# A feed-forward kernel whose weight sums move from GpSimd to VectorE, and whose residual comes in half tiles

## The chip, the cores and the metric

The kernel runs on one core of a Trainium2 chip. The metric is the device time of one execution in microseconds (us), as the median of several runs. The core's engines are TensorE (PE in the profile, its weight loads PEld), VectorE (DVE), ScalarE (ACT), GpSimd (POOL) and SyncE (SP, which here only issues DMAs). Each engine takes its instructions in order from a queue of its own and waits where an instruction's input isn't there or the buffer that it writes isn't free. A DMA is issued from the queue of an engine, in that engine's order.

## The reference, cut to what matters

One layer (`DEPTH = 1`): a spatial-gating mixer and a cross-attention side by side, a projection, a LayerNorm with a scaled residual, then a SwiGLU feed-forward with another residual and LayerNorm. Only the feed-forward and its residual bear on the change.

```python
D_MODEL = 1024; SEQ = 2048; D_FF = 2816
DEEPNORM_ALPHA = (2 * DEPTH) ** 0.25

def swiglu_ffn(x, w_in, w_down):
    h = x @ w_in
    return (jax.nn.silu(h[..., :D_FF]) * h[..., D_FF:]) @ w_down

x = layer_norm(DEEPNORM_ALPHA * x + branch @ w_o[i], ln1_g[i], ln1_b[i])
x = layer_norm(DEEPNORM_ALPHA * x + swiglu_ffn(x, ffn_w_in[i], ffn_w_down[i]), ln2_g[i], ln2_b[i])
```

## The kernel before

**Numbers.** Every operand of a matmul is split into a high part and the rest: `split` (L70 to L74) casts it on ScalarE to the type of TensorE's inputs (L73, the high part) and subtracts the result from it on VectorE (L74, the low part). Each product is then three matmuls (`PASSES`: high by high, high by low, low by high). So no weight reaches TensorE before ScalarE and VectorE have both worked on it. Blocks of 2 by 2 submatrices are multiplied with seven products in place of eight; this needs sums of the submatrices made ahead, on both sides, and sums of the products behind.

**Passes and blocks.** The feed-forward works on the tokens in three passes of 688, 680 and 680 (`FPASSES`), each in two halves of `h` = 344 or 340. The 2816 hidden features are 22 columns f of 128, taken in five blocks: 5, 4, 4, 4, 5 of them in pass 0, and 4, 4, 4, 4, 6 in passes 1 and 2 (`FBLOCKS`). For each f, `up(f)` multiplies x by w1 (84 matmuls of 128x344 or 128x340, tile `h`); behind the products 5, 7, 3 and 4 VectorE takes the results out of PSUM (L401, L402, L392, L396), and the result `c` is split into `g`. After its columns, the block's part of the product with w2 is added to the output tiles `fa`.

**The products with w2.** In pass 0, `down` does this with plain products (tile `d`). In passes 1 and 2, the first four blocks use seven products (`down7`, tile `e`, weights `w_e`). What these need of w2 is made once, in pass 0, by the generator `left_sums` (L484): for each of the first four blocks (`blk`) and each pair of output rows (`m` = 0, 2, 4, 6), 16 tiles in all. One tile is worked on during each `up(f)` of pass 0 from f = 5, a step behind each product. Its steps are: two DMAs from GpSimd's queue load the tile `r_es..m` (L481, in `tiles4`); four sums of 128x256 into `s_es..m` (L493); then for each of two parts a split (L73, L74) and a store to device memory from GpSimd's queue (L499, `k_e`). `r_es` and `s_es` share the pool `g` with the tiles g, 7 buffers.

**The residual.** In passes 1 and 2, `down7` adds the residual in its fourth block (`last`), since the fifth block is done by `down`. This is in `second(j)`, for j = 0 to 3: an add of a common part into the output tile (L531, L532), then for each of two row tiles m a load of x1d (128x680, tile `r_fr`, L538, SP's queue) into the pool tag `raw`, and `fa = ALPHA * r + fa` on VectorE (L539). The tag `raw` has 4 buffers (L66, `raw`) and serves nearly every weight that is loaded, among them `r_u_17_0`, the weight of `up(17)`, the first work of TensorE behind the fourth block. The pool `tmp` (L888) has 9 buffers of 128 by `h`; each `up(f)` takes five of them:

```python
def tmp(self, name):
    return open_pools["tmp"].tile([P, self.h], F32, tag="tmp", name=f"{name}_{self.no}")

m1, u2, c12, c21, c22 = (self.tmp(f"{x}_{f}") for x in ("m1", "u2", "c12", "c21", "c22"))
```

**What sets the order.** The program is written by a framework whose scheduler puts each engine's instructions in an order from its own estimates; only the order of TensorE is fixed by hand (`in_order`). An edit of one instruction can move others on every engine.

Of the kernel before, what the change touches and what calls it, by code (L numbers as in the profile page):

```python
# [14 lines left out]
ALU = mybir.AluOpType  # L15
AX = mybir.AxisListType

P = 128
# [16 lines left out]
ALPHA = 2.0 ** 0.25  # L35
# [4 lines left out]
def trunk_kernel(ctx, tc, xT, memT, wv, wuq, ws, bs, vg, vb, wmk, wmv, wo,  # L40
                 ln1g, ln1b, w1, w2, ln2g, ln2b, outT):
    nc = tc.nc
# [16 lines left out]
    def matmul(*args, **kw):  # L59
        in_order(nc.tensor.matmul(*args, **kw))  # L60
# [4 lines left out]
    def bank(name):  # L65
        return psum.tile([P, 512], F32, tag="bank", name=name)  # L66

    def raw(shape, name):
        return common.tile(shape, F32, tag="raw", bufs=4, name=name)

    def split(hi, lo, src, engine=nc.vector):

        nc.scalar.copy(hi, src)  # L73
        engine.tensor_sub(lo, src, hi.bitcast(F32))  # L74
# [109 lines left out]
    x1d = dram.tile([D, SEQ], F32, tag="x1d", name="x1d")  # L184
# [160 lines left out]
    class Pass:  # L345
# [138 lines left out]
        def left_sums(self, blk, m, f0, q):  # L484

            name, key = f"es{blk}_{m}", f"e{blk}_{m}"
            r, s = (open_pools["g"].tile([P, 4, q, P], F32, tag="g", name=f"{x}_{name}") for x in "rs")
            v = self.tiles4(m, f0, q, name, r.rearrange("p (a i) j x -> p a (i j) x", a=2))
            yield
            a11, a12, a21, a22 = (v[:, a, j] for a in range(2) for j in range(2))  # L490
            for n, (x, y, op) in enumerate(((a21, a22, ALU.add), (s[:, 0], a11, ALU.subtract),
                                            (a11, a21, ALU.subtract), (a12, s[:, 1], ALU.subtract))):
                nc.gpsimd.tensor_tensor(out=s[:, n], in0=x, in1=y, op=op)  # L493
                yield
            for pa, k, to in ((5, slice(0, 2), r), (7, slice(2, 4), s)):
                hl = to.bitcast(F32R)
                split(hl[:, 0:2], hl[:, 2:4], s[:, k])
                t = kept[f"{key}_{pa}"] = dram.tile([P, 4, q, P], F32, tag=f"{key}_{pa}", name=f"k_{key}_{pa}")
                nc.gpsimd.dma_start(out=t, in_=to)  # L499
                yield  # L500

        def down7(self, blk, q, f0, last, w):

            h, n, gp = self.h, self.n, self.gp
            if blk == 0:
                self.u = [open_pools["sums"].tile([P, 4, P], F32, tag="sums", name=f"fu{self.no}_{m}")
                          .rearrange("p a b -> p (a b)")[:, 0:h] for m in range(0, KD, 2)]
            banks = []

            def product(j, p):  # L510
                y, u = self.out[j], self.u[j]
                c11, c12, c21, c22 = (y[:, a, b * h:(b + 1) * h] for a in range(2) for b in range(2))
                n, start, stop = {1: (0, True, False), 6: (1, True, True), 2: (0, False, True), 5: (2, True, False),
                                  7: (3, True, False), 3: (2, False, True), 4: (3, False, True)}[p]
                bk = banks[j][n]
                for i in range(q):
                    for x, (a, b) in enumerate(PASSES):
                        matmul(bk, w[j][p][:, a, i, :], gp[p][:, i, b], start=start and i == 0 and x == 0,
                               stop=stop and i == q - 1 and x == 2, skip_group_check=True)
                to = {1: u, 6: u, 2: c11, 5: c22, 7: c22, 3: c12, 4: c21}[p]  # L520
                if blk == 0 and p not in (1, 7):
                    nc.scalar.copy(to, bk)
                else:
                    nc.vector.tensor_add(to, to, bk)

            def second(j):
                for p in (2, 3, 4):
                    product(j, p)
                if last:
                    y, u = self.out[j], self.u[j]  # L530
                    nc.vector.tensor_add(y[:, 0, h:n], y[:, 0, h:n], u)  # L531
                    nc.vector.tensor_tensor(out=y[:, 1].rearrange("p (b t) -> p b t", b=2),  # L532
                                            in0=y[:, 1].rearrange("p (b t) -> p b t", b=2),
                                            in1=u.unsqueeze(1).broadcast_to([P, 2, h]), op=ALU.add)
                    for m in range(2):
                        r = raw([P, n], f"r_fr{self.no}_{j}_{m}")
                        m0 = (2 * j + m) * P
                        nc.sync.dma_start(out=r, in_=x1d[m0:m0 + P, self.t0:self.t0 + n])  # L538
                        nc.vector.scalar_tensor_tensor(out=y[:, m], in0=r, scalar=ALPHA, in1=y[:, m],  # L539
                                                       op0=ALU.mult, op1=ALU.add)  # L540

            for j in range(KD // 2):
                if j < KD // 2 - 1:
                    w.append(self.left(blk, 2 * j + 2, f0, q))
                banks.append([bank(f"e{i}_{self.no}_{blk}_{j}")[:, 0:h] for i in range(4)])
                for p in (6, 1, 5, 7):
                    product(j, p)
                if j:
                    second(j - 1)
            second(KD // 2 - 1)  # L550

        def sums(self):
# [427 lines left out]
    for no in range(len(FPASSES)):  # L980
        pa, h, n = ffn, FPASSES[no] // 2, FPASSES[no]
# [136 lines left out]
```

## Time and profile before

| | |
|---|---|
| Median of three runs | 2203.02 us |
| The three runs | 2204.48, 2203.02, 2201.71 us |
| The profiled execution | 2201.52 us, span 2199.7 us |
| Mean granted clock of TensorE | 0.987 |
| DMA | 408.12 MB, mean 186 GB/s |
| Costliest group: the `h` matmuls | 5544 of mean 322 ns, 892.5 us |

The span is the time from the first to the last instruction in the trace. The profile lists for each group of instructions the line of the source, the engine, the operation, the tile written and the tiles read (without their numbers), with count, busy time and the idle time just before them, and what ended it. In a timeline a row is a run of equal instructions: start, length from the first start to the last end, what it is, how many, and in brackets the idle time before it and who ended it. Names after an arrow are who was waited for. A row `DMA r_es<-in_w` says that the landing of that load was awaited.

### The profile page before, as it was taken

How to read it: one execution, taken by the hardware profiler on the slowest of the kernel's cores; microseconds unless marked ns; L12 is line 12 of the kernel's file. 1: busy time of each engine (PE TensorE's matmuls, PEld its weight loads, DVE VectorE, ACT ScalarE, POOL GpSimd, SP SyncE). 2: the span in 40 equal slices, each digit the busy share in tenths (PEclk: the TensorE clock that was granted, in tenths of full speed). 3: DMA queues.
4: the chain of work that ended last, by engine and by line, in shares of the span. 5: the costliest groups of instructions: out<-in, count | busy, mean ns of one | idle time of the engine just before them, and what ended most of it. 6: DMA issues, size and time to landing. Idle time of an engine off the chain costs nothing.

```text
span 2199.7 us, 35087 instructions
## 1 busy us (share of the span) xinstructions
PE 2097.4 (95%) x12938; PEld 1983.4 (90%) x12938; DVE 1591.2 (72%) x2950; ACT 921.4 (42%) x1846; POOL 419.8 (19%) x382
## 2 busy tenths in 40 slices
PE   9999999999999989999999999999989999999896
PEld 7888798798788879998999999999989999999896
DVE  7987796797788795776767875666757765666656
ACT  5553743654465452433424445332224353223234
POOL 1412321331322441213222320000002300000002
PEclk9999999999999999999999999999999999999998
DMA  6233324234334555767667558666674576666752
GB/s 211 77 115 125 106 79 161 91 97 147 118 96 132 187 198 217 256 207 275 215 227 276 168 198 268 222 227 229 224 246 141 197 262 236 231 230 218 249 168 94
DMA packets 156299, 408.12 MB, mean 186 GB/s; under 512 B 15328, under 2 KB 41952, under 8 KB 156128
## 3 DMA queue, kind: packets, MB, share of 16 engines
q1 hardware_dynamic: 135808, 333.50, 45.5%
q10 hardware_dynamic: 12672, 46.14, 5.4%
q0 software_dynamic: 7648, 26.24, 3.5%
q8 instruction: 102, 1.67, 0.3%
q14 instruction: 69, 0.57, 0.1%
HBM read 326.13 MB, written 79.69 MB: 184 GB/s over the span
## 4 chain that ended last, share of the span: by engine, by line
PE 62%; DVE 16%; DMA 8%; ACT 5%; issue 5%; POOL 4%; SPq 0%; ACTq 0%; DVEq 0%; POOLq 0%
PE h L60 30%; PE d L60 10%; PE e L60 9%; PE v L60 5%; PE y L60 4%; PE u L60 3%; DMA r_es<-in_w 2%; DMA r_x<-in_xT 2%; DVE w L74 1%; POOL s_es L493 1%; DVE w_u L74 1%; DVE w_o L74 1%; POOL s_a L233 1%; POOL s_b L233 1%; ACT p L743 1%
## 5 line engine op out<-in xcount | busy, mean ns | idle before, releaser
L60 PE MATMUL h<-x,w 128*128 128x340 f32 (+1 forms) x5544 | 892.5, 322 | 48.2 <-DVE c L401 17.2
L60 PEld LDWEIGHTS h<-x,w 128*128 128x128 f32 x5544 | 876.9, 190 | 59.6 <-ACT w L73 31.9
L60 PE MATMUL d<-g,w_d 128*128 128x344 f32 (+3 forms) x1632 | 264.0, 322 | 8.4 <-DVE g L74 3.6
L60 PEld LDWEIGHTS d<-g,w_d 128*128 128x128 f32 x1632 | 257.9, 189 | 12.7 <-DVE g L74 5.3
L60 PE MATMUL y<-br,w_o 128*128 128x512 f32 x960 | 224.2, 395 | 0.0
L60 PEld LDWEIGHTS y<-br,w_o 128*128 128x128 f32 x960 | 180.6, 189 | 41.7
L60 PE MATMUL e<-gp,w_e 128*128 128x340 f32 x1344 | 211.4, 318 | 0.0
L60 PEld LDWEIGHTS e<-gp,w_e 128*128 128x128 f32 x1344 | 209.9, 188 | 0.5 <-DVE w_e L74 0.2
L73 ACT CAST w<-r_u 128x512 fp32r<-128x512 f32 x198 | 121.8, 618 | 191.1 <-PE h L60 126.2
L60 PE MATMUL v<-w_v,x 128*128 128x512 f32 x768 | 187.8, 401 | 6.6 <-ACT w_v L73 4.8
L74 DVE TENSOR_TENSOR w<-r_u,w 128x512 fp32r<-128x512 f32 x198 | 144.2, 730 | 53.9 <-ACT w L73 46.6
L60 PEld LDWEIGHTS v<-w_v,x 128*128 128x128 f32 x768 | 143.5, 190 | 42.1 <-ACT w_v L73 4.8
L369 POOL TENSOR_TENSOR t<-r_f,r_f 128x340 f32<-128x340 f32 (+1 forms) x12 | 13.4, 1113 | 441.2 <-DVE c L392 377.0
L60 PE MATMUL u<-xt,w_u 128*128 128x256 f32 x768 | 97.1, 282 | 0.0
L60 PEld LDWEIGHTS u<-xt,w_u 128*128 128x128 f32 x768 | 94.3, 191 | 0.0
L60 PE MATMUL u<-x,w_u 128*128 128x256 f32 x576 | 79.5, 290 | 10.5 <-DVE u L709 5.2
L73 ACT CAST w_d<-r_d 128x384 fp32r<-128x384 f32 (+2 forms) x104 | 53.0, 519 | 76.4 <-PE d L60 50.7
L74 DVE TENSOR_TENSOR w_o<-r_o,w_o 128x512 fp32r<-128x512 f32 (+1 forms) x96 | 69.3, 732 | 21.4 <-ACT w_o L73 21.4
L60 PEld LDWEIGHTS u<-x,w_u 128*128 128x128 f32 x576 | 72.9, 193 | 13.1 <-issue 5.1
L74 DVE TENSOR_TENSOR w<-s_u,w 128x512 fp32r<-128x512 f32 x88 | 67.6, 775 | 22.0 <-ACT w L73 20.2
L73 ACT CAST gp<-c 128x340 fp32r<-128x340 f32 x112 | 51.8, 476 | 74.6 <-DVE c L398 42.0
L400 DVE TENSOR_TENSOR u<-h,m 128x340 f32<-128x340 f32 (+1 forms) x66 | 33.7, 511 | 66.9 <-PE h L60 65.9
(212 smaller groups left out, 2901.1 us busy)
## 6 DMA issues: line engine op xcount, KB each, us to landing
w<-k_u SPq DMA_DIRECT2D x176, 512.0 KB, 4.3
r_u<-in_w SPq DMA_DIRECT2D x88, 512.0 KB, 3.7
k_u<-w ACTq DMA_DIRECT2D x88, 512.0 KB, 3.3
r_u<-in_wuq SPq DMA_DIRECT2D x32, 512.0 KB, 3.3
r_o<-in_wo SPq DMA_DIRECT2D x32, 512.0 KB, 3.5
r_e<-in_w SPq DMA_DIRECT2D x64, 256.0 KB, 3.2
w_e<-k_e SPq DMA_DIRECT2D x64, 256.0 KB, 3.6
w_e<-k_e SPq DMA_DIRECT2D x32, 512.0 KB, 4.3
```

Of the source, the lines that this page charges most:

```text
L60: in_order(nc.tensor.matmul(*args, **kw))
L73: nc.scalar.copy(hi, src)
L74: engine.tensor_sub(lo, src, hi.bitcast(F32))
L233: nc.gpsimd.tensor_add(self.s2, self.s2, sq)
L369: nc.gpsimd.tensor_sub(t3, b22, b12)
L400: stages = {1: lambda: nc.scalar.copy(m1, q0), 6: lambda: nc.vector.tensor_add(u2, q1, m1), 2: lambda: nc.scalar.activation(m1, q0, AF.Sil ...
L493: nc.gpsimd.tensor_tensor(out=s[:, n], in0=x, in1=y, op=op)
L743: nc.scalar.activation(pr[:, h, :], svs[h // 2][:, h % 2, :], AF.Exp, scale=HD ** -0.5, bias=mxv[:, h:h + 1], accum_out=sm[:, h:h + 1])
```

## The change

Two edits. The four sums of `left_sums` are made by VectorE in place of GpSimd; the loads and stores of these tiles stay in GpSimd's queue. And in `second`, each residual tile of 128x680 in `raw` becomes two half tiles of 128x340 in `tmp`, each with its own load and its own instruction of VectorE. Lines from L540 on move down by two.

```diff
             for n, (x, y, op) in enumerate(((a21, a22, ALU.add), (s[:, 0], a11, ALU.subtract),
                                             (a11, a21, ALU.subtract), (a12, s[:, 1], ALU.subtract))):
-                nc.gpsimd.tensor_tensor(out=s[:, n], in0=x, in1=y, op=op)
+                nc.vector.tensor_tensor(out=s[:, n], in0=x, in1=y, op=op)
                 yield
...
                     for m in range(2):
-                        r = raw([P, n], f"r_fr{self.no}_{j}_{m}")
                         m0 = (2 * j + m) * P
-                        nc.sync.dma_start(out=r, in_=x1d[m0:m0 + P, self.t0:self.t0 + n])
-                        nc.vector.scalar_tensor_tensor(out=y[:, m], in0=r, scalar=ALPHA, in1=y[:, m],
-                                                       op0=ALU.mult, op1=ALU.add)
+                        for x in range(2):
+                            r, t0 = self.tmp(f"r{m}{x}_{j}"), self.t0 + x * h
+                            nc.sync.dma_start(out=r, in_=x1d[m0:m0 + P, t0:t0 + h])
+                            to = y[:, m, x * h:(x + 1) * h]
+                            nc.vector.scalar_tensor_tensor(out=to, in0=r, scalar=ALPHA, in1=to,
+                                                           op0=ALU.mult, op1=ALU.add)
```

The order of the instructions moves with it. First VectorE in pass 0, in the block of f = 9 to 12, beside the tile of m = 4. In the names, `c_11` is the result of `up(11)`, `r_es_4` and `s_es_4` are the tile of m = 4, `w_0_12` are weights of `up(12)`, and `s_u` sums for them. Before:

```order
L74 TENSOR_TENSOR w_0_11_9971<-r_u_11_1_9843,w_0_11_9971 128x512
L135 TENSOR_TENSOR s_u_12_10015<-r_u_12_0_10007,r_u_12_1_10008 128x512
L136 TENSOR_TENSOR s_u_12_10016<-r_u_12_0_10007,s_u_12_10012 128x512
L401 TENSOR_TENSOR c_11_0_9841<-h_0_11_9835,u_11_0_9838 128x344
L74 TENSOR_TENSOR r_es_4_9870<-s_es_4_9871,r_es_4_9870 128x512
L402 TENSOR_TENSOR c_11_0_9841<-h_0_11_9836,c_11_0_9841 128x344
L74 TENSOR_TENSOR w_0_12_10019<-r_u_12_0_10007,w_0_12_10019 128x512
L74 TENSOR_TENSOR s_es_4_9871<-s_es_4_9871 128x512
```

After:

```order
L74 TENSOR_TENSOR w_0_11_9971<-r_u_11_1_9843,w_0_11_9971 128x512
L493 TENSOR_TENSOR s_es_4_9871<-r_es_4_9870 128x256 x2
L493 TENSOR_TENSOR s_es_4_9871<-s_es_4_9871,r_es_4_9870 128x256
L135 TENSOR_TENSOR s_u_12_10015<-r_u_12_0_10007,r_u_12_1_10008 128x512
L401 TENSOR_TENSOR c_11_0_9841<-h_0_11_9835,u_11_0_9838 128x344
L493 TENSOR_TENSOR s_es_4_9871<-r_es_4_9870,s_es_4_9871 128x256
L136 TENSOR_TENSOR s_u_12_10016<-r_u_12_0_10007,s_u_12_10012 128x512
L74 TENSOR_TENSOR w_0_12_10019<-r_u_12_0_10007,w_0_12_10019 128x512
L402 TENSOR_TENSOR c_11_0_9841<-h_0_11_9836,c_11_0_9841 128x344
L74 TENSOR_TENSOR r_es_4_9870<-s_es_4_9871,r_es_4_9870 128x512
```

Three sums now stand ahead of L401 and the fourth behind it, and the split of `r_es_4` has gone from ahead of L402 to behind it.

Then the same queue one column later, beside the tile of m = 6 and the products of `up(12)`. Before:

```order
L74 TENSOR_TENSOR w_0_12_10113<-s_u_12_10016,w_0_12_10113 128x512
L74 TENSOR_TENSOR r_es_6_10035<-s_es_6_10036,r_es_6_10035 128x512
L401 TENSOR_TENSOR c_12_0_10006<-h_0_12_10000,u_12_0_10003 128x344
L74 TENSOR_TENSOR w_0_12_10136<-r_u_12_1_10008,w_0_12_10136 128x512
L402 TENSOR_TENSOR c_12_0_10006<-h_0_12_10001,c_12_0_10006 128x344
L74 TENSOR_TENSOR s_es_6_10036<-s_es_6_10036 128x512
```

After:

```order
L74 TENSOR_TENSOR w_0_12_10113<-s_u_12_10016,w_0_12_10113 128x512
L74 TENSOR_TENSOR w_0_12_10136<-r_u_12_1_10008,w_0_12_10136 128x512
L493 TENSOR_TENSOR s_es_6_10036<-r_es_6_10035 128x256 x2
L493 TENSOR_TENSOR s_es_6_10036<-s_es_6_10036,r_es_6_10035 128x256
L493 TENSOR_TENSOR s_es_6_10036<-r_es_6_10035,s_es_6_10036 128x256
L401 TENSOR_TENSOR c_12_0_10006<-h_0_12_10000,u_12_0_10003 128x344
L74 TENSOR_TENSOR r_es_6_10035<-s_es_6_10036,r_es_6_10035 128x512
L402 TENSOR_TENSOR c_12_0_10006<-h_0_12_10001,c_12_0_10006 128x344
```

L401 stands behind the four sums here, no longer behind the split of `r_es_6`; the last split of the weights of `up(12)` has come ahead of both.

At last SP's queue at the fourth block of pass 1, up to the load of `r_u_17`, the weights of `up(17)`. `w_e_3_6` and `r_e_3_6` are the weights for the block's last two output rows, `r_fr` the residual tiles. Before:

```order
L481 DMA r_e_3_6_16055<-in_w 128x512 x2
L465 DMA w_e_3_6_16060<-k_e_6_7_12004 128x2x256
L472 DMA w_e_3_6_16069<-k_e_6_7_12004 128x2x256
L538 DMA r_fr_1_0_16126<-x1d 128x680
L538 DMA r_fr_1_1_16129<-x1d 128x680
L538 DMA r_fr_2_0_16187<-x1d 128x680
L538 DMA r_fr_2_1_16190<-x1d 128x680
L538 DMA r_fr_3_0_16216<-x1d 128x680
L538 DMA r_fr_3_1_16219<-x1d 128x680
L141 DMA r_u_17_0_16236<-in_w 128x1024
```

After (the half tiles are named `r_j`):

```order
L481 DMA r_e_3_6_16061<-in_w 128x512 x2
L90 DMA w_e_3_6_16064<-k_e_6_5_11982 128x1024
L472 DMA w_e_3_6_16075<-k_e_6_7_12004 128x2x256
L539 DMA r_1_1_16141<-x1d 128x340
L465 DMA w_e_3_6_16066<-k_e_6_7_12004 128x2x256
L539 DMA r_2_1_16199<-x1d 128x340
L539 DMA r_2_1_16202<-x1d 128x340
L539 DMA r_2_1_16205<-x1d 128x340
L141 DMA r_u_17_0_16260<-in_w 128x1024
L142 DMA r_u_17_1_16261<-in_w 128x512
L539 DMA r_2_1_16208<-x1d 128x340
```

Behind the loads of `r_e_3_6`, six residual loads of a whole tile stood ahead of `r_u_17_0`; now four of a half tile do.

## The prediction, made before the changed kernel was run

> **What bounds the kernel now.** I read the page first: who is busy, and on which engines the chain that ended last runs.
>
> ```profile
> span 2199.7 us, 35087 instructions
> PE 2097.4 (95%) x12938; PEld 1983.4 (90%) x12938; DVE 1591.2 (72%) x2950; ACT 921.4 (42%) x1846; POOL 419.8 (19%) x382
> ```
>
> TensorE works 2097.4 of 2199.7 us, so at most some 100 us can go without changing its work, and what counts is where TensorE stops. The sums of the change are made while the first pass multiplies x by w1 (product tile `h`) and by w2 (`d`), from about 815 to 1210 us. The view of waits, TensorE only, that stretch (waited for: us in total, times, longest):
>
> ```profile
> PE h L60 <- DVE c L401: 12.6, 6, 2.7
> PE d L60 <- ACT g L73: 3.2, 3, 2.2
> PE d L60 <- DVE g L74: 3.0, 4, 0.9
> PE h L60 <- ACT w L73: 2.5, 1, 2.5
> PE h L60 <- DVE c L402: 1.5, 2, 0.8
> ```
>
> The first and last rows, 14.1 us, say that TensorE waits for VectorE to take a product out of PSUM (L401, L402). The windows (length, then busy time of PE, PEld, DVE, ACT, POOL, granted clock, DMA share, GB/s) show that these stops lie in one short stretch of each of the four later blocks:
>
> ```profile
> 900.00:940.00 40.00, 36.07 (x217) 35.28 (x216) 29.05 (x54) 17.79 (x35) 13.20 (x20) 0.96 0.80 284
> 1000.00:1030.00 30.00, 24.99 (x154) 23.96 (x154) 19.15 (x37) 12.45 (x25) 10.82 (x16) 1.00 0.77 270
> 1088.00:1118.00 30.00, 25.66 (x158) 24.53 (x157) 21.80 (x38) 12.88 (x25) 12.05 (x16) 1.00 0.77 272
> 1178.00:1210.00 32.00, 27.77 (x165) 27.18 (x164) 23.60 (x41) 13.87 (x27) 10.40 (x14) 0.95 0.77 284
> ```
>
> TensorE is idle for 3.9, 5.0, 4.3 and 4.2 us in them, 17.5 us together. VectorE is idle too (10.9 of 30 us in the second), so it isn't short of time there: something blocks it. The second stretch on TensorE:
>
> ```profile
> 1006.02 11.57 PE L60 MATMUL h<-x,w 128*128 128x344 f32 x72 [0.82 <-DVE c L402]
> 1020.33 4.03 PE L60 MATMUL h<-x,w 128*128 128x344 f32 x24 [2.74 <-DVE c L401]
> ```
>
> There are two stops: 0.82 us beside the sums of m=4 (tile `es..4`), 2.74 us beside those of m=6. A product is 12 matmuls, 11.57/6 = 1.93 us. Now the chain behind the stops, in the timelines of that stretch. GpSimd sums the tile of m=4:
>
> ```profile
> 1000.63 1.93 POOL L493 TENSOR_TENSOR s_es<-r_es 128x256 f32<-128x256 f32 x2 [7.49 <-DMA r_es<-in_w]
> 1002.53 0.73 POOL L493 TENSOR_TENSOR s_es<-s_es,r_es 128x256 f32<-128x256 f32 x1
> 1003.34 0.74 POOL L493 TENSOR_TENSOR s_es<-r_es,s_es 128x256 f32<-128x256 f32 x1
> ```
>
> It issues the load for m=6 and waits 6.21 us for its landing:
>
> ```profile
> 1007.91 1.08 POOL L481 DMA_DIRECT2D r_es<-in_w  x2
> 1015.20 1.69 POOL L493 TENSOR_TENSOR s_es<-r_es 128x256 f32<-128x256 f32 x2 [6.21 <-DMA r_es<-in_w]
> ```
>
> VectorE, first beside m=4, then beside m=6 (in brackets its idle time and what ended it):
>
> ```profile
> 1004.76 0.69 DVE L74 TENSOR_TENSOR r_es<-s_es,r_es 128x512 fp32r<-128x512 f32 x1 [2.80 <-ACT r_es L73]
> 1005.37 0.51 DVE L402 TENSOR_TENSOR c<-h,c 128x344 f32<-128x344 f32 x1
> ```
>
> ```profile
> 1014.91 0.69 DVE L74 TENSOR_TENSOR w<-s_u,w 128x512 fp32r<-128x512 f32 x1 [2.39 <-ACT w L73]
> 1019.07 0.69 DVE L74 TENSOR_TENSOR r_es<-s_es,r_es 128x512 fp32r<-128x512 f32 x1 [3.47 <-ACT r_es L73]
> 1019.67 0.51 DVE L401 TENSOR_TENSOR c<-h,u 128x344 f32<-128x344 f32 x1
> ```
>
> So the m=6 stop runs: the load lands at 1015.20, GpSimd sums for 3.4 us, ScalarE casts, VectorE has waited 3.47 us for that cast and splits at 1019.07, only then does L401 run, and TensorE starts at 1020.33. VectorE is blocked by an instruction that has nothing to do with TensorE's next product but stands ahead of L401 in its queue.
>
> **Part 1, the sums on VectorE.** Removed: 64 sums of GpSimd (16 tiles of 4), 1.93 + 0.73 + 0.74 = 3.4 us for a tile of four. Added: the same 64 on VectorE. A sum of this shape on VectorE stands elsewhere in the trace:
>
> ```profile
> 546.66 0.76 DVE L653 TENSOR_TENSOR s<-r_x 128x256 f32<-128x256 f32 x2 [2.52 <-DMA r_x<-in_xT]
> 547.34 0.42 DVE L653 TENSOR_TENSOR s<-r_x,s 128x256 f32<-128x256 f32 x1
> ```
>
> The second starts 0.68 us after the first pair: 0.34 a sum in a run, 1.4 for four, 64 × 0.34 = 22 us in all. By the order after, L401 no longer stands behind GpSimd, ScalarE's cast and the split, but behind the four sums alone.
>
> Term 1, beside m=4. The load lands at 1000.6. Then by the new order: three sums to 1001.7, L135 (0.6 in a run) 1002.3, L401 1002.8, the fourth sum 1003.1, L136 and a split of w 1004.3, L402 done at about 1004.9. TensorE ended the product before at 1006.02 − 0.82 = 1005.2, so the wait goes. Next late is TensorE's product into L401's bank, due at 1005.2 − 1.93 = 1003.3: 0.5 us of room. The four stops of this kind are 14.1 − 4 × 2.74 = 3.1 us (3.2 from the single rows); I leave 0.5 in all: **−2.7**.
>
> Term 2, beside m=6. The load is issued behind the store of the m=4 sums, whose last split moves back by about 0.3 us (1006.39 + 0.69 before): it lands near 1015.4. Sums to 1016.8, L401 to 1017.3, with the semaphore TensorE starts at 1017.5. It is free at 1020.33 − 2.74 − 0.8 = 1016.8. A wait of 0.8 takes the place of 2.74: 4 × 1.95 = **−7.8**. Next late is the load itself.
>
> Term 3, the starts of the down products: the `d` rows of the waits, 6.2 us, of which one of 2.2 us is another matter (it is no L401 stretch), and about 3.4 follow the late L401 by the splits of `g`. Between 0 and 3.4, half: **−1.7**.
>
> Term 4, the granted clock behind a stop (windows: length, PE, PEld, DVE, ACT, POOL, clock):
>
> ```profile
> 930.50:936.00 5.50, 5.44 (x25) 5.47 (x26) 4.37 (x8) 2.72 (x7) 1.96 (x4) 0.71 0.83 282
> 1020.30:1024.30 4.00, 3.97 (x25) 4.00 (x26) 3.74 (x7) 1.82 (x5) 1.93 (x4) 1.00 0.83 273
> 1198.80:1206.00 7.20, 7.12 (x35) 7.15 (x36) 6.49 (x13) 3.87 (x8) 0.91 (x2) 0.76 0.87 301
> ```
>
> Of three 2.74-us stops, two are followed by a low clock. What it costs: 24 matmuls took 4.03 us in the second window at full clock; at 0.71 the first needs 5.44, +1.4; the third loses 7.12 × 0.24 = 1.7. Between 0 and 3.1, half, since shorter stops remain: **−1.5**. [...]
>
> Term 5, what the added work displaces. Three of a block's four tiles are summed beside the `h` products: 12 × 0.34 = 4.1 us, next to idle time on VectorE of 2.80 + 2.39 + 3.47 = 8.7 us in the shown block. It fits in sum but not at every place: between 0 and 4 × 1.0 (a sum pushing a split by 0.34 three times a block), I take 0.5 a block: **+2.0**. What is queued behind a sum that waits for its load is all of VectorE, the splits of w for the next products included.
>
> Something speaks for a gain on VectorE instead. The same instruction in two blocks:
>
> ```profile
> 999.98 0.68 DVE L135 TENSOR_TENSOR s_u<-r_u,r_u 128x512 f32<-128x512 f32 x1
> ```
>
> ```profile
> 1089.63 1.22 DVE L135 TENSOR_TENSOR s_u<-r_u,r_u 128x512 f32<-128x512 f32 x1
> ```
>
> In the second GpSimd was summing at that time, in the first it was not yet. [...]
>
> **Part 2, the residual in half tiles.** Passes 1 and 2, behind the fourth block, where `up(17)` starts: TensorE in both, then SP's queue and VectorE in pass 1.
>
> ```profile
> 1602.38 0.93 PE L60 MATMUL h<-x,w 128*128 128x340 f32 x2 [6.78 <-ACT w L73]
> 1603.65 2.62 PE L60 MATMUL h<-x,w 128*128 128x340 f32 x8 [0.33 <-DVE w L74]
> ```
>
> ```profile
> 2058.32 0.93 PE L60 MATMUL h<-x,w 128*128 128x340 f32 x2 [5.68 <-ACT w L73]
> ```
>
> ```profile
> 1585.14 9.88 SPq L538 DMA_DIRECT2D r_fr<-x1d  x6
> 1596.36 0.33 SPq L141 DMA_DIRECT2D r_u<-in_w  x1
> ```
>
> ```profile
> 1600.50 1.64 DVE L539 SCALAR_TENSOR_TENSOR fa<-r_fr,fa 128x680 f32<-128x680 f32 x2
> 1602.06 0.94 DVE L74 TENSOR_TENSOR g<-c,g 128x340 fp32r<-128x340 f32 x2
> 1602.90 1.29 DVE L74 TENSOR_TENSOR w<-r_u,w 128x512 fp32r<-128x512 f32 x2
> ```
>
> Before, the weight tile of `up(17)` is issued at 1596.36, behind six residual loads that wait for `raw` buffers; with landing, ScalarE casts near 1602. After, the order puts it behind four half loads, which wait in `tmp` alone; it comes some 10 us earlier and is no longer the limit. Added: 8 more load issues and 8 more VectorE instructions a pass, in halves: 2 × 0.45 for one of 0.82, next to nothing. Next late is VectorE: the third matmul needs the low half of w, and that split stands behind the whole end of the block. TensorE ends it at 1602.38 − 6.78 = 1595.6. Then: an add and L531 (0.5 each, as half the `g` row), L532 (0.85, one 128x680), four halves 1.8, `g` 0.94, split 0.68: 5.3 us, with hand-overs 1601.5 instead of 1603.65: −2.1. In the last pass the wait is 1.1 shorter (5.68): −1.2. Term 6: **−3.3**, between 0 (VectorE's end hides it) and −2 × 5 (if the splits of w went first).
>
> **Sum.** −2.7 − 7.8 − 1.7 − 1.5 + 2.0 − 3.3 = −15.0, on the profiled execution of 2201.52 us (span 2199.7): 2186.5. The median of the runs, 2203.02, lies 1.5 higher, as should the new one: **2188.0**.
>
> **The rivals.**
> 1. Nothing changes within what counts. The m=4 and m=6 loads bound the cycle: POOL waited 7.49 and 6.21 us for them, and a wait for the load simply moves from GpSimd to VectorE. For it: it is the longest wait of the chain. Against: between landing (1015.20) and L401 (1019.67) lie 4.5 us of which the new order needs 1.4. Landing 1.9 us later (15/8 places) would undo the gain: with part 2's end hidden as well, 2199 to 2205.
> 2. **Slower**: VectorE takes its queue in order, and its sums now wait for the load with everything behind them. At eight places (m=4 and m=6, four blocks) a load that lands x us later stops TensorE x us longer, since the cover is only 0.5 us at m=4 and gone at m=6. Loads wait for stores, stores for splits that now stand later, so x feeds on itself. It decides above 15/8 = 1.9 us; at 2.5 us it is +5: 2208.
> 3. More: terms 1 to 4 in full (another 0.5 + 3.2 + 1.7 + 1.6) and no term 5 (2.0): 9 more, 2179.
> 4. Part 2 does nothing because VectorE's end of the block hides the earlier weights, and terms 3 and 4 stay: 2188 + 6.5 = 2194.5, up to 2198 with part of a wait left at m=6.
>
> **How the numbers follow.** Forecast with its terms (2181 to 2195): 0.56. Rival 3: 0.07. Rival 4 beyond 2195: 0.09. Rival 1: 0.18. Rival 2: 0.10. 0.2% is 4.4 us, about what a measurement of this kernel tells from no change: faster 0.56 + 0.07 + 0.09 = 0.72, same 0.18, slower 0.10. The range goes from rival 3's 2179 to 2202, the middle of rival 1; outside lie rival 2, half of rival 1 and a little of rival 3, 0.2 together.
>
> **What would show it.** Right: no `DVE c L401` wait above 1 us on TensorE between 900 and 1210 us, the four windows' idle time down from 17.5 to about 6; no low clock behind them; VectorE's waits there named `DMA r_es`; TensorE's wait at `up(17)` some 2 us shorter and ended by `DVE w` alone; VectorE's busy time up by at most 22 us. Wrong: those waits stay at 2 us or more with the load landing later than 7.3 us after its issue (1007.91 to 1015.20), or new stops for `ACT w` or `DVE w` among the `h` products.

## The result

The changed kernel takes 2186.41 us (2183.62 to 2188.79, four runs), the kernel before beside it 2203.75 us: a ratio of 0.9918, 95% interval 0.9899 to 0.9938 (the quotient of the two medians, 0.9921, lies inside). Measured again beside the experiments it was 0.9913 (0.9896 to 0.9929). The forecast was 2188.0, within 2179 to 2202.

The head of the page after:

```profile
span 2186.7 us, 35143 instructions
## 1 busy us (share of the span) xinstructions
PE 2094.2 (96%) x12938; PEld 1982.2 (91%) x12938; DVE 1606.3 (73%) x3030; ACT 920.8 (42%) x1846; POOL 365.2 (17%) x318
```

VectorE works 15 us more and GpSimd 55 us less, and the span is 13.0 us shorter. TensorE's waits from 815 to 1230 us, the view shown of before, whole:

```profile
PE h L60 <- DVE c L401: 4.5, 4, 1.8
PE h L60 <- ACT w L73: 2.5, 1, 2.5
PE d L60 <- ACT g L73: 2.2, 1, 2.2
PE d L60 <- DVE g L74: 0.3, 1, 0.3
```

L401 and L402 together fell from 14.1 to 4.5 us, the `d` starts from 6.2 to 2.5 us. VectorE's own waits in the same stretch say what stood ahead of L401: before, it waited 28.4 us in front of splits of `r_es` for ScalarE's cast; after, 2.2 us there, and 9.0 us for the load. Before, then after:

```profile
DVE r_es L74 <- ACT r_es L73: 28.4, 11, 3.5
```

```profile
DVE s_es L493 <- DMA r_es<-in_w: 9.0, 5, 2.9
...
DVE r_es L74 <- ACT r_es L73: 2.2, 7, 0.7
```

The windows of the four blocks, at about the same places of the program:

```profile
900.00:940.00 40.00, 39.41 (x249) 38.87 (x248) 35.47 (x72) 20.08 (x39) 6.49 (x12) 1.00 0.85 296
997.00:1027.00 30.00, 28.19 (x179) 27.78 (x178) 24.56 (x49) 13.08 (x26) 4.32 (x8) 1.00 0.82 290
1081.00:1111.00 30.00, 29.32 (x186) 28.94 (x185) 25.03 (x50) 14.68 (x29) 4.32 (x8) 1.00 0.84 299
1165.00:1197.00 32.00, 30.59 (x194) 30.25 (x194) 27.54 (x55) 16.15 (x33) 3.24 (x6) 1.00 0.84 310
```

TensorE's idle time in them is 0.6, 1.8, 0.7 and 1.4 us in place of 17.5 in all, and the granted clock is 1.00 in each. VectorE beside m=4 and m=6 of the second block (the timeline; the last row but one is L401):

```profile
999.47 0.76 DVE L493 TENSOR_TENSOR s_es<-r_es 128x256 f32<-128x256 f32 x2 [0.28 <-DMA r_es<-in_w]
...
1015.32 0.76 DVE L493 TENSOR_TENSOR s_es<-r_es 128x256 f32<-128x256 f32 x2 [2.91 <-DMA r_es<-in_w]
1016.00 0.42 DVE L493 TENSOR_TENSOR s_es<-s_es,r_es 128x256 f32<-128x256 f32 x1
1016.45 0.42 DVE L493 TENSOR_TENSOR s_es<-r_es,s_es 128x256 f32<-128x256 f32 x1
1016.79 0.51 DVE L401 TENSOR_TENSOR c<-h,u 128x344 f32<-128x344 f32 x1
1017.56 0.69 DVE L74 TENSOR_TENSOR r_es<-s_es,r_es 128x512 fp32r<-128x512 f32 x1 [0.26 <-ACT r_es L73]
```

At m=6, VectorE now waits for the load itself, 2.91 us, and L401 ends 2 us behind the landing; before, it ended 5 us behind (1015.20 to 1020.18). The stop that is left is the one forecast at this place, 1.81 us in place of 0.8.

The table has the length of three stages, between the starts of TensorE's runs in the timelines: pass 0 from `up(5)` to the first matmul of pass 1, and in passes 1 and 2 the fourth block's products with `up(17)` and the rest of the columns, to the first `d`. All kernels of the experiments are in it, in us. Each row of lengths is one profiled execution; each ratio is taken from all runs, against the kernel before run beside it.

| kernel | pass 0, f = 5 to 21 | fourth block, pass 1 | fourth block, pass 2 | ratio to before, 95% interval |
|---|---|---|---|---|
| before | 380.7 | 101.0 | 100.6 | 1 |
| the change | 363.0 | 99.9 | 99.6 | 0.9918 (0.9899 to 0.9938) |
| the change again | 363.8 | 99.1 | 100.0 | 0.9913 (0.9896 to 0.9929) |
| sums alone | 364.0 | 100.3 | 101.1 | 0.9911 (0.9895 to 0.9928) |
| residual alone | 382.0 | 98.9 | 99.5 | 0.9983 (0.9974 to 0.9992) |
| sums of m = 0, 2 | 383.4 | 101.0 | 101.1 | 1.0008 (0.9999 to 1.0017) |
| sums of m = 4, 6 | 364.5 | 104.5 | 101.2 | 0.9920 (0.9906 to 0.9935) |
| loads from ScalarE's queue | 388.6 | 99.9 | 98.8 | 1.0005 (0.9993 to 1.0016) |
| residual ahead | 364.4 | 98.7 | 97.7 | 0.9900 (0.9885 to 0.9915) |
| splits on GpSimd too | 393.0 | 101.0 | 101.6 | 1.0068 (1.0052 to 1.0083) |
| residual ahead, load early | 358.3 | 97.8 | 97.1 | 0.9869 (0.9848 to 0.9890) |
| residual ahead, loads from SP's queue | 372.7 | 97.1 | 97.5 | 0.9925 (0.9909 to 0.9940) |
| sums twice | 387.6 | 99.2 | 99.7 | 1.0001 (0.9986 to 1.0016) |
| before, load early | 375.3 | 101.2 | 101.1 | 0.9971 (0.9961 to 0.9981) |

Pass 0 got 17.7 us shorter and the two fourth blocks 2.1 us. Pass 0 as one window, before and after:

```profile
877.60:1258.30 380.70, 360.96 (x2246) 356.32 (x2245) 284.73 (x508) 153.79 (x300) 97.39 (x131) 0.99 0.65 230
```

```profile
882.20:1245.10 362.90, 355.88 (x2245) 353.16 (x2245) 297.48 (x568) 152.62 (x300) 47.66 (x73) 1.00 0.68 241
```

TensorE's idle time fell from 19.7 to 7.0 us, by 12.7, and the same matmuls took 5.1 us less. The profiled execution shows only 13.0 us in all, less than the 19.8 of the stages, because the other 6.8 us were lost elsewhere in this pair of executions. 4.6 us of them lie ahead of `up(5)` (882.17 beside 877.61), and 4.4 of these ahead of the first `h` matmul (754.37 beside 749.96), up to which every queue holds the same instructions in the same order; so this part is scatter and no effect of the change. The remaining 2.2 us lie in the stages that the table leaves out. The other kernels' executions reach `up(5)` between 875.1 and 884.0 us.

### The profile page after: what moved, and what is told of

Its sections match the earlier page's. It is cut to its first block, busy times and chain, and to the rows that moved or that the text cites. A ratio compares the mean times of both kernels' runs of the same rounds, so it can differ in the third digit from the quotient of the medians.

```text
span 2186.7 us, 35143 instructions
## 1 busy us (share of the span) xinstructions
PE 2094.2 (96%) x12938; PEld 1982.2 (91%) x12938; DVE 1606.3 (73%) x3030; ACT 920.8 (42%) x1846; POOL 365.2 (17%) x318
## 4 chain that ended last, share of the span: by engine, by line
PE 58%; DVE 19%; DMA 10%; ACT 5%; issue 5%; POOL 2%; SPq 0%; ACTq 0%; DVEq 0%; POOLq 0%
PE h L60 31%; PE e L60 9%; PE d L60 8%; PE v L60 5%; PE u L60 3%; DMA r_x<-in_xT 3%; DMA r_f<-x1d 2%; DMA r_es<-in_w 2%; DVE w L74 2%; DVE w_o L74 2%; DVE x L74 1%; DVE w_u L74 1%; POOL s_a L233 1%; ACT p L745 1%; DVE z L702 1%
## 5 line engine op out<-in xcount | busy, mean ns | idle before, releaser
L60 PE MATMUL u<-xt,w_u 128*128 128x256 f32 x768 | 97.1, 282 | 0.0
L400 DVE TENSOR_TENSOR u<-h,m 128x340 f32<-128x340 f32 (+1 forms) x66 | 33.7, 511 | 70.7 <-PE h L60 70.3
L74 DVE TENSOR_TENSOR w_d<-r_d,w_d 128x384 fp32r<-128x384 f32 (+2 forms) x104 | 61.9, 599 | 24.5 <-ACT w_d L73 24.3
```

Source lines behind the costliest of these rows:

```text
L400: stages = {1: lambda: nc.scalar.copy(m1, q0), 6: lambda: nc.vector.tensor_add(u2, q1, m1), 2: lambda: nc.scalar.activation(m1, q0, AF.Sil ...
```

## The experiments

Theory Q, from the prediction: VectorE was blocked, in the order of its queue, by splits of r_es that waited for GpSimd and ScalarE. Rival C, for contention: GpSimd's sums slowed VectorE's own instructions. Each diff is against the kernel named; where none is, against before.

**The parts by themselves.** Sums alone and residual alone are the two halves of the diff.

> Only the 64 sums on VectorE, the residual as before. Theory Q (queue): VectorE was blocked by splits that stood ahead of L401 and L402 and waited for GpSimd and ScalarE; the gain lies in pass 0 between 875 and 1250 us, TensorE loses its L401 waits from 14 to about 4.5 us there, and the time is 14 to 18 us less than before (about 2188). Theory C (contention): GpSimd's sums made VectorE's own instructions slow; same total here, told apart by the next kernels. If the residual were the larger part instead, this would be under 8 us.

> Only the residual in half tiles, the sums on GpSimd. My theory: the weights of up(17) come early in both passes, but VectorE's end of the block bounds the third matmul: TensorE's restart is 2 us and 1.3 us earlier, and a part of it is lost again to a lower clock behind it; 1 to 3 us less than before in all. Rival: the early weights count in full, 6 us or more. A second rival: nothing, within 1 us.

The whole again, beside later kernels:

> The whole change once more, beside the next kernels on one chip. If its two parts add up, 0.989 of before by the two parts' ratios (0.9911 x 0.9983 = 0.9894, 2185 beside 2208); by the first measurement 0.9918. A ratio of 0.9911 or more would say that the residual part gives nothing beside the sums.

The sums alone give 0.9911, the residual alone 0.9983, the whole 0.9913 and 0.9918. The sums are nearly all of it. The residual is worth 3.8 us by itself (0.0017 of 2208.5), more than I expected by a little, and 2 to 3 us in the stages of the table; beside the sums it is within the intervals, and by the mark set ahead of the repeat (0.9911 or more) it gives nothing there that these runs can tell.

**Which sums.**

```diff
-                nc.gpsimd.tensor_tensor(out=s[:, n], in0=x, in1=y, op=op)
+                (nc.vector if m in (0, 2) else nc.gpsimd).tensor_tensor(out=s[:, n], in0=x, in1=y, op=op)
```

The second kernel has (4, 6) in that place.

> The sums of m=0 and m=2 on VectorE (half of the 64), those of m=4 and m=6 on GpSimd, the residual as before. Q: the tiles of m=0 and m=2 stop TensorE nowhere, so -3 to +1 us. C: half of the sums bring half of the gain, about -8 us.

> The sums of m=4 and m=6 on VectorE, those of m=0 and m=2 on GpSimd, the residual as before. Q: nearly the whole gain of the sums, -13 to -17 us. C: half of it, about -8 us.

1.0008 for m = 0, 2 and 0.9920 for m = 4, 6. The half that stands beside stops brings the whole gain, the other half none. C as an even slowing falls: half of the sums did not bring half of the gain. A slowing that counts only beside the stops would look the same in these two kernels; against it stand VectorE's waits above (28.4 us in front of the splits) and the kernel below in which the L401 waits go although GpSimd sums. TensorE's waits with m = 0, 2 on VectorE are those of before:

```profile
PE h L60 <- DVE c L401: 12.6, 5, 2.7
```

**Where the load is issued.** Against the change:

```diff
-            queue = nc.sync if r is None else nc.gpsimd
+            queue = nc.sync if r is None else nc.scalar
```

> The change, with the loads of r_es issued from ScalarE's queue in place of GpSimd's (the stores stay with GpSimd). Theory: what is left of the L401 waits (4.5 us) is set by the landing, 8.7 us behind the issue for m=6; from ScalarE's queue the issue comes some 2 us later but a transfer of this kind lands in 3.3 us, so the waits fall to under 1.5 us and the time by 2 to 5 us below the change. Rival: ScalarE's queue holds the loads back behind casts that wait, VectorE's sums wait longer with all behind them, and the time rises by 2 to 8 us.

The rival held: 1.0005, all of the gain lost. TensorE's and VectorE's waits:

```profile
PE h L60 <- DVE w L74: 18.4, 14, 2.8
...
PE h L60 <- DVE c L401: 0.6, 1, 0.6
```

```profile
DVE s_es L493 <- DMA r_es<-in_w: 19.2, 11, 3.5
```

The L401 waits did go, but VectorE waits 19.2 us for the load in place of 9.0, and what stands behind it now are splits of w. In the second block ScalarE issued the second half of the m=6 load at 1011.69, behind casts of `g`, where GpSimd had issued both at 1006.61 to 1007.69; the sums started at 1016.40, 6.3 us behind the first issue (1010.06) in place of 8.7, so the transfer was quicker but started later. With the loads in SP's queue (`queue = nc.sync`, on the kernel with the residual ahead, below), the same, milder:

> The kernel with the residual ahead, and the loads of r_es issued from SP's queue (the stores stay with GpSimd). SP's loads stand behind loads of weights that wait for raw buffers, and these behind the loads of r_es in turn. By the theory that a late load stops all of VectorE: where a load comes later than from GpSimd's queue TensorE gets new stops, for w or for L401, 5 to 20 us in all (ratio 0.992 to 0.999). Rival: SP's shorter landing (3.2 us beside 5.4) counts more, ratio 0.986 to 0.989.

```profile
DVE s_es L493 <- DMA r_es<-in_w: 22.8, 14, 3.3
```

```profile
PE h L60 <- DVE c L401: 9.2, 6, 2.6
```

Ratio 0.9925 beside 0.9900 without this edit; the intervals overlap, but pass 0 is 8.3 us longer (372.7 beside 364.4), and TensorE's L401 waits were 5.1 us without it. The rival's premise fell too. The 5.4 us that I had for a load from GpSimd's queue was the median of loads and stores together, and the 3.2 us belonged to loads of another stage: these loads alone took 6.5 us (median) from GpSimd's queue and 6.1 from SP's, where they now stand.

**VectorE out of the chain.** GpSimd makes the low halves too:

```diff
-                split(hl[:, 0:2], hl[:, 2:4], s[:, k])
+                split(hl[:, 0:2], hl[:, 2:4], s[:, k], nc.gpsimd)
```

> The kernel before, with the low half of the split of r_es and s_es made by GpSimd too: VectorE has no part in this work, and GpSimd has 32 more instructions of 128x512 that read two tiles. Theory Q: VectorE cannot be blocked by it any more; the L401 waits go for the most part, but ScalarE's casts still wait for GpSimd, with the casts of w behind them, so TensorE waits for w instead by 1 to 2 us at m=6: 4 to 12 us below before. Theory C: more GpSimd work slows VectorE more: at or above before.

1.0068, so my expectation failed. ScalarE, then VectorE:

```profile
1012.63 0.62 ACT L73 CAST r_es<-s_es 128x512 fp32r<-128x512 f32 x1 [4.48 <-POOL s_es L493]
1013.15 0.61 ACT L73 CAST w<-r_u 128x512 fp32r<-128x512 f32 x1
```

```profile
1013.80 1.34 DVE L74 TENSOR_TENSOR w<-r_u,w 128x512 fp32r<-128x512 f32 x1 [3.72 <-ACT w L73]
```

VectorE is blocked all the same, by a split of w that waits for ScalarE, which waits for GpSimd: ScalarE is a relay. L402 stands behind it. TensorE's waits for L402 are 12.0 us, and those at the starts of `d`, for ScalarE's cast of `g`, are 12.7 us where they were 3.2:

```profile
PE d L60 <- ACT g L73: 12.7, 4, 3.6
PE h L60 <- DVE c L402: 12.0, 8, 2.4
```

The split itself takes 1.34 us in place of 0.68, beside a GpSimd split (1013.32, 1.27 us). Which of the two, relay or contention, costs more here this run does not tell.

**Twice the work.** Each sum is made twice, against the change (`for _ in range(2):` around it).

> The change, with each of the 64 sums made twice by VectorE (22 us more work for it, same values). If VectorE has room, as I charged 2 us for the first 64, only the sums beside the stops count: 1.4 us more at m=6 and up to 0.7 at m=4 in four blocks, 3 to 8 us above the change (ratio 0.9925 to 0.995). If VectorE's busy time is what bounds pass 0: 15 to 22 us, back at before. If the sums cost nothing at all: within 1.5 us of the change (0.9905 to 0.992).

1.0001: some 20 us, where I expected 3 to 8; that is the size that the rival of a full VectorE had. But pass 0 as one window shows VectorE busy 316 of 388 us, so it is not full; what it waits for most is the load:

```profile
883.10:1270.70 387.60, 365.24 (x2247) 360.32 (x2246) 316.17 (x627) 154.45 (x300) 47.64 (x73) 0.98 0.65 226
```

```profile
DVE s_es L494 <- DMA r_es<-in_w: 23.3, 9, 4.4
```

It was 9.0 us with the sums made once, and TensorE's waits for L401 are 15.2 us in place of 4.5. A load is issued behind a store of the tile before, this behind a split, this behind the sums: what delays the sums comes back as a later load, and all of VectorE waits for it. That the delay returns in this way is read from the trace; no run took the loop away with the sums doubled.

**The load early.** On the kernel with the residual ahead (below), the generator of the next tile is made at the end of `up(f)` and its load issued there, ahead of the two stores of the tile before:

```diff
-            if no == 0 and f > 4 and sums_to_make:
-                blk, m = sums_to_make.pop(0)
-                work.append((pa.left_sums(blk, m, 4 * blk, 2), 1))
+            if loaded:
+                work.append((loaded.pop(), 1))
...
             side.clear()
+            if no == 0 and f > 3 and sums_to_make:
+                blk, m = sums_to_make.pop(0)
+                loaded.append(pa.left_sums(blk, m, 4 * blk, 2))
+                next(loaded[0])
             return ys
```

> The kernel with the residual ahead (0.9900 of before), and each load of r_es issued at the end of the up before, ahead of the two stores of the tile before it in GpSimd's queue. Theory: what is left of the stops in pass 0 (4 to 5 us of L401) is the landing of the load behind those stores; some 10 us earlier it has landed when VectorE comes to the sums. L401 waits under 1.5 us, VectorE's waits for the load under 2 us, ratio 0.986 to 0.989. Rival: the sums are now placed earlier in VectorE's queue and wait for the load there, with splits of w behind them: 0.990 or more.

0.9869, 2178.26 us: as expected, and the fastest kernel here. The interval just touches that of the kernel without the early load (0.9885 to 0.9915); pass 0 is 6.1 us shorter (358.3 beside 364.4). The view of waits has no L401, no L402 and no `DMA r_es` any more.

**The same with the sums on GpSimd.** The same diff on the kernel before.

> The kernel before (sums on GpSimd, whole residual tiles), with each load of r_es issued at the end of the up before, as in the last experiment but three. The splits still stand ahead of L401 in VectorE's queue, and GpSimd still takes 3.4 us for a tile. Theory: what stops VectorE is that this chain comes late, not which engine sums; with the load early GpSimd has done when VectorE comes to the split, the L401 waits go from 14 to under 4 us, pass 0 (the two later stages of f=5 to 21) gets 14 to 20 us shorter, ratio 0.990 to 0.994. [...]

0.9971: pass 0 is 5.4 us shorter where theory Q had 14 to 20. The L401 waits are gone, as Q said:

```profile
PE h L60 <- ACT m L400: 6.9, 6, 1.7
PE d L60 <- DVE g L74: 4.7, 5, 1.6
PE d L60 <- ACT g L73: 3.0, 3, 2.2
PE h L60 <- DVE c L402: 2.9, 2, 1.5
```

But others have come. VectorE and GpSimd at one place:

```profile
1008.44 3.02 DVE L74 TENSOR_TENSOR w<-s_u,w 128x512 fp32r<-128x512 f32 x1
```

```profile
1008.77 1.45 POOL L493 TENSOR_TENSOR s_es<-r_es 128x256 f32<-128x256 f32 x2
1010.17 0.74 POOL L493 TENSOR_TENSOR s_es<-s_es,r_es 128x256 f32<-128x256 f32 x1
1010.85 0.58 POOL L481 DMA_DIRECT2D r_es<-in_w  x1
1011.45 0.76 POOL L493 TENSOR_TENSOR s_es<-r_es,s_es 128x256 f32<-128x256 f32 x1
```

A split of 0.68 us takes 3.02 and ends half a microsecond behind the third of the four sums (1010.91). The groups by form, from 880 to 1240 us, say it for all (count, busy us, mean ns); before, the change, this kernel:

```profile
L74 DVE TENSOR_TENSOR w<-s_u,w 128x512 fp32r<-128x512 f32 x66 | 46.1, 705 | 13.5 <-ACT w L73 11.7
```

```profile
L74 DVE TENSOR_TENSOR w<-s_u,w 128x512 fp32r<-128x512 f32 x67 | 45.2, 686 | 4.7 <-ACT w L73 2.9
```

```profile
L74 DVE TENSOR_TENSOR w<-s_u,w 128x512 fp32r<-128x512 f32 x67 | 55.0, 830 | 5.2 <-ACT w L73 3.4
```

From the split of 3.02 us one of the new stops can be followed in the rows. L392, which takes a product out of PSUM, starts only behind it (1011.38), ScalarE waits 2.59 us for L392, and TensorE then stops for a copy that stands further back in ScalarE's queue (`m`, L400):

```profile
1011.92 0.49 ACT L393 ACTIVATE c<-c 128x344 f32<-128x344 f32 x1 [2.59 <-DVE c L392]
```

```profile
1015.56 9.71 PE L60 MATMUL h<-x,w 128*128 128x344 f32 x60 [1.22 <-ACT m L400]
```

So C is real, and the kernel before hid it: there GpSimd summed while VectorE stood still and waited for it (mean 705 beside 686 ns). Take that wait away and the sums fall on VectorE's work. How much of the lost gain C makes up is not shown: one stop was followed, not all. Nor does any kernel leave the sums on GpSimd and only put the split behind L401.

**The residual ahead.** Against the change, in `second`, the products 2, 3 and 4 come behind the block of the residual:

```diff
             def second(j):
-                for p in (2, 3, 4):
-                    product(j, p)
                 if last:
...
+                for p in (2, 3, 4):
+                    product(j, p)
```

> The change, with the residual and the common part added ahead of the last three products of a pair of rows in place of behind them (the same sums in another order). Theory: TensorE's 5.5-us wait at up(17) is VectorE's end of the fourth block; of the 4.5 us behind the last product only the three adds, g and w stay, so the wait falls to about 3 us in both passes, with less of a clock loss behind it: 4 to 7 us below the change. Rival: the load of the residual or the weights is what ends last, and the wait stays at 5 us or more: within 1.5 us of the change.

0.9900 beside 0.9913 on the same chip; the medians differ by 3.1 us, less than expected, and the intervals overlap. TensorE's restart in pass 1, the change, then this kernel:

```profile
1589.41 22.77 PE L60 MATMUL h<-x,w 128*128 128x340 f32 x133 [5.55 <-DVE w L74]
```

```profile
1586.04 39.21 PE L60 MATMUL h<-x,w 128*128 128x340 f32 x234 [3.94 <-DVE w L74]
```

The wait falls by 1.6 us (4.19 in pass 2), not by 2.5: VectorE's end of the block does bound it, but the last three adds (L524) stay there.

## Why the prediction was right

The mechanism was right and so was its place; that the sum came out so near is in part luck, because its parts erred in both directions. In the stages of the table the gain is 19.8 us where the sum had 15.0; by the medians it is 17.3. Of the signs, one missed: L401 waits of 1.81 and 1.41 us stayed where none above 1 us was to stay.

- **Terms 1 and 2** (−10.5 for the stops at L401 and L402): 14.1 to 4.5 us, −9.6. The stops beside m=4 went in the first three blocks, but 1.41 us stayed in the fourth, where the sums wait 2.29 us for their load. Those beside m=6 became 0.59, 1.81, 0.68 and none. That m = 4, 6 alone bring the gain shows the place; the load early shows that the rest is the landing, as "next late is the load itself" had it.
- **Term 3** (−1.7 for the starts of `d`): 6.2 to 2.5 us, −3.7: it came in full, where I took half.
- **Term 4** (−1.5 for the clock): mis-sized, it came in full. By the two slow rows of before it was worth 5.44 × 0.29 + 7.12 × 0.24 = 3.3 us, and in the rest of pass 0 the clock was 1.00. Behind the fourth stop of 2.74 us (1108.90), which the prediction does not weigh, the clock was 1.00 too. The 24 matmuls behind the stop of the first block took 5.45 us before; now

```profile
932.00 4.02 PE L60 MATMUL h<-x,w 128*128 128x344 f32 x24 [0.59 <-DVE c L401]
```

  and the clock was 1.00 in all four windows. No stop that was left here, up to 1.81 us, lowered it; that was not sure, since in the kernel with the residual alone a stop of 1.80 us had a clock of 0.58 in the 4 us behind it. TensorE's busy time fell by 5.1 us, 1.8 more than the clock explains. Most of that is the ends of its runs, an estimate: pass 0 has 7 stops in place of 16, and a matmul counts 0.32 us but starts 11.57/72 = 0.16 us behind the one before it in a run, so each stop less takes 0.16 us of busy time with it.
- **Term 5** (+2.0 for added work): this step failed as a picture. The view of waits has no new row that would be its loss. But the room was not free either: a second set of sums cost some 20 us, not 2. I had priced a sum by its 0.34 us and the splits that it pushes; at a place with slack it showed no cost, and where there is none it also makes the next load later, as read from the trace of the doubled sums. The prediction had this loop only in its slower rival ("x feeds on itself").
- **Term 6** (−3.3 for the residual): the step behind it was right. The third matmul came 1.8 and 1.5 us sooner against the start of its block, 3.3 together, `DVE w` ends the wait, and the tail runs as listed, but for three adds where one was listed. The term left out what lies behind that matmul. TensorE stood for 6.78 us ahead of the first two matmuls before; now it starts these two, stands for 5.55 us, and the window from the third matmul on runs slower than before (the change, then before):

```profile
1589.40:1597.00 7.60, 7.59 (x37) 7.59 (x38) 1.76 (x3) 1.29 (x3) 0.00 (x0) 0.74 0.38 138
```

```profile
1603.60:1611.00 7.40, 7.35 (x40) 7.36 (x41) 1.80 (x3) 1.72 (x4) 0.00 (x0) 0.83 0.84 299
```

  From the third matmul to the first `d`, without a stop, the same products took 67.0 us in place of 66.4, and in pass 2 67.4 in place of 66.9. So 2.1 us were left of 3.3.
- **The rivals.** The slower one didn't happen here: the m=6 load of the second block landed 48.9 us behind the block's first `h` matmul, before 48.3, so 0.6 us later where 1.9 would have undone the gain. It took 8.7 us from its issue in place of 7.3, but was issued 0.8 us earlier in the block. The rival's mechanism is what undid the gain with the loads in ScalarE's queue and, as read from the trace, with the sums doubled. Of the gain on VectorE that the row of 1.22 us for 0.68 spoke for, a part came: by the two windows of pass 0, 60 sums were added, some 20 us at 0.34, and VectorE is busy 12.8 us more, so some 8 us came back, an estimate. It was no more because GpSimd's sums had fallen in VectorE's waits: by the timelines of before, VectorE was idle in about half of the some 50 us in which GpSimd summed in pass 0.

## What to carry to other kernels

When an engine idles in front of a row that has nothing to do with what comes next, read its queue and not its load: here VectorE had time to spare, and what counted was a split that stood ahead of L401 and waited for two other engines. Before moving such work to the blocked engine, look where its input comes from and issue that earlier: the move gave 0.9 per cent, the load issued early another 0.3, and the early load without the move only 0.3, at least in part because the helper's work then fell on the engine that it was meant to spare (830 ns for a split on the mean, 705 before). Slack in the sum of a stage is not slack at a place: the first 22 us of work on VectorE showed no cost of their own, the second cost some 20.

## What the hardware showed that I had not expected

- With the sums on GpSimd and the load early, one VectorE instruction took 3.02 us for 0.68 while GpSimd made three sums beside it; the longest of this shape in pass 0 of before was 1.23.
- The length of a stop alone did not settle TensorE's clock behind it. Behind the four stops of 2.74 us before, it was 0.71, 1.00, 1.00 and 0.76 (windows of 4 to 7 us); behind a stop of 1.81 us of the change 1.00, and behind one of 1.80 us with the residual alone 0.58; behind one of 5.55 us 0.74.
- The first 750 us, with the same instructions in the same order, differ by up to 6.0 us between executions (749.96 to 756.01 at the first `h` matmul), a third of the effect studied; only lengths of stages, not times from the start, could be compared between profiles.
